# Four heads' output gates moved into the Strassen gate pairs, and the row sums moved to GpSimd

## The chip, the cores and the metric

The program runs on one core of one Trainium2 chip. The metric is the device time of one execution in microseconds (us). Times are medians of several runs; the profile is of one further execution.

In the rows below PE is TensorE's matmul, PEld its weight load, DVE is VectorE, ACT is ScalarE, POOL is GpSimd and SP is SyncE, which here only issues DMAs. "Granted clock" is the share of TensorE's full clock that the chip allowed.

## The reference, cut to what matters

One layer of a hybrid model over 1,280 tokens (1,024 latent and 256 context tokens), width D = 1024, all in float32:

```python
u   = rmsnorm(x, g_norm1) * (1 + sc1) + sh1
xp, su, sv, q, k, v, o_pre, gate_pre, br_pre = split(u @ w_in)
y_a = pool_branch(xp)                                # centred window means, a linear map per group
y_b = su * (w_sgu applied per chunk to rmsnorm(sv))  # spatial gating
h   = mlstm(q, k, v, gate_pre)                       # 4 heads of 128 channels, both directions
h   = rmsnorm_per_head(h) * g_mlstm
y_c = sigmoid(o_pre) * h                             # the output gate of the heads
merged = sum_r sigmoid(br_pre[r]) * (y_r @ w_branch[r])
x  += gt1 * (merged @ w_out)
x  += gt2 * relu(rmsnorm(x)*(1+sc2)+sh2 @ w_ff1)**2 @ w_ff2
```

The change concerns `o_pre` (512 columns of `w_in`, 128 for each head), `br_pre` (3 x 1024 columns) and where `sigmoid(o_pre)` meets `h`.

## The kernel before, in words

Every float32 product is made of three matmuls on rounded parts: a value is split into `hi` (rounded to the matmul's format, by ACT) and `lo` (the rest, by DVE), and hi x hi, hi x lo and lo x hi are summed in PSUM. The modulated input `u` stays on chip, transposed: `uT[k][g]` for 8 blocks k of 128 channels and 3 token groups g of 512, 512 and 256 tokens (the last one is the context).

The stages in order of time:

- Start, 0 to 84 us: modulation, transposes, and the first projections, with an order written out by hand.
- Gate chain, about 84 to 142 us: the heads' input and forget gates, a serial chain of ACT and DVE instructions on 36 partitions (lines 435 to 490, in rows of the tile `z`), then transposes `pc` (line 498).
- Heads, about 142 to 450 us: `head(h)` for h = 0 to 3. Each transposes k and v (`tk`, `tv`), runs the state scan (`kv`, line 607 on DVE), and then for each token group g the scores `st`, the decay rows `rb`, the weights `w` and `e` (lines 635 to 645), the products `pv` (lines 654 and 656), a normalisation whose power is done by POOL (`rs_h`, line 130), the transposes `th` (line 671) and `yc`, which goes to memory. `head_proj(h + 1)` makes the next head's k, v and q with `proj` and `dense` (matmuls of lines 123 to 125, tiles `p_k`, `p_v`, `p_q`); these do not depend on `head(h)` and run between its instructions. So does `proj(I_O + h, ...)` (tile `p_o`), whose sigmoid (line 617) is kept in `so`, a region of `z`, until `yc` is made (line 673).
- After the heads, 450 to 559 us: `sv`'s normalisation, pooling (`pool_project`, `pool_window`, `pool_out`), spatial gating (`spatial`). `quarter_sums` reads `u` back from memory (`scr_u`) into `z` and makes sums of its quarters on DVE (line 800); `split_sum` splits them (lines 809 and 810).
- Gate pairs, 559 to 858 us: 12 objects `GatePair`, each for two blocks of 128 columns of `br_pre`. A pair treats its 256 columns and the 1,024 latent tokens as 2 x 2 blocks and forms them with Strassen's seven block products: `B11`, `B21`, `B22` with parts of `uT` itself, and `T1` to `T4` with the split sums. The context tokens are multiplied in the ordinary way (`contexts`). In between, `mod_piece` multiplies and adds rows of `w_ada` on DVE (lines 539 and 541), 64 pieces, no more than 6 for each pair so far.
- Branches, 858 to 1026 us: for each r, `y_r` is read from memory and split, multiplied by `w_branch[r]` and by the stored gate.
- Output projection, feed-forward with Strassen products, final norm: to 1941 us.

The order of instructions on each engine is that of the program's own scheduler, which runs a model of the engines when the kernel is built (`schedule_with_timeline_sim=True`); it may bring an instruction that is ready ahead of earlier code. Only the start is pinned. Each engine then runs its queue in that fixed order. Tiles of 128 x 512 (`slot`) come from a pool of 59; `uT` holds 40 of them.

Of the kernel before, what the change touches and what calls it, by code (L numbers as in the profile page):

```python
# [7 lines left out]
F32 = mybir.dt.float32  # L8
# [13 lines left out]
H = 4  # L22
# [26 lines left out]
def hybrid_step(  # L49
# [503 lines left out]
    vaug = z[:, 1280:2570].rearrange("p (c t) -> p c t", t=129)  # L553
    vs = z[:, 2570:5150].rearrange("p (c d t) -> p c d t", d=2, t=129)
    S = z[:, 5150:7730].rearrange("p (c d t) -> p c d t", d=2, t=129)
    so = z[:, 7730:9010]
    hn2 = [z[:, 9010 + i * 512 : 9522 + i * 512].rearrange("p (c t) -> p c t", t=P) for i in range(2)]

    def proj(idx, name, evict, eng=V, w=None, groups=range(3)):
# [15 lines left out]
    def head(h, kT, vT, qT):  # L575
# [36 lines left out]
            V.scalar_tensor_tensor(fin[:, d, :], S[:, nx, d, :], dc(nx, d), kv(nx, d), ALU.mult, ALU.add)  # L612
        A.dma_start(st_out[h], fin)

        def ev_o(g, ps):
            t0, n = GROUPS[g]
            A.activation(so[:, t0 : t0 + n], ps[:, :n], AF.Sigmoid)

        ssq = small([P, 16], f"ssq{h}")
        for g in range(3):  # L620
            t0, n = GROUPS[g]
# [41 lines left out]
                V.scalar_tensor_tensor(hn[:, cl, :], pvv[:, 1, 0:P], den[:, 1, :], hn[:, cl, :], ALU.mult, ALU.add)  # L663
                A.activation(vs[:, c, 0, 0:P], hn[:, cl, :], AF.Square, accum_out=ssq[:, c : c + 1])
            r = rstd_of(ssq[:, c0 : c0 + ncn], ncn, f"h{h}_{g}")
            if g == 0:
                proj(I_O + h, f"o{h}", ev_o)
            ps = ps_sd(f"th{h}_{g}")
            for cl in range(ncn):
                A.activation(hn[:, cl, :], hn[:, cl, :], AF.Copy, scale=r[:, cl : cl + 1])  # L670
                PE.transpose(ps[:, cl * P : (cl + 1) * P], hn[:, cl, :], ident)  # L671
            yc = tmp(f"yc{h}_{g}")
            V.scalar_tensor_tensor(  # L673
                yc[:, :n], ps[:, :n], ccol[:, C_GM + h : C_GM + h + 1], so[:, t0 : t0 + n], ALU.mult, ALU.mult)
# [116 lines left out]
    SUMS = {"T1": "B11", "T3": "B12", "T2": "B22", "T4": "B21"}  # L791

    def quarter_sums(raw):
        for kk in range(4):
            b11, b21, b12, b22 = raw["B11"][kk], raw["B21"][kk], raw["B12"][kk], raw["B22"][kk]
            if raw is u_raw:
                for t, k, g in ((b11, kk, 0), (b12, kk, 1), (b22, kk + 4, 1), (b21, kk + 4, 0)):
                    SP.dma_start(t, scr_u[g][k])
            for out, x, y in ((b11, b12, b11), (b12, b22, b12), (b22, b22, b11), (b21, b22, b21)):
                V.tensor_tensor(out, x, y, ALU.subtract)  # L800

    def split_sum(dst, raw, nm):
        for kk in range(4):
            t = raw[SUMS[nm]][kk]
            if nm == "T2" and kk < 3:
                hi, lo = (six(f"t2{i}{kk}") for i in "hl")
            else:
                hi, lo = slot(f"{nm}h{kk}"), slot(f"{nm}l{kk}")
            A.copy(hi, t)
            V.tensor_tensor(lo, t, hi.bitcast(F32), ALU.subtract)  # L810
            dst[nm, kk] = hi, lo

    us = {}
    u_raw = {
        nm: [zs(i) for i in at]
        for nm, at in (("B21", (0, 1, 2, 3)), ("B22", (4, 5, 6, 7)), ("B12", (8, 9, 10, 11)), ("B11", (12, 13, 16, 17)))}
# [45 lines left out]
    pool_out(1)  # L862
    spatial(2)
    pool_out(0)
    quarter_sums(u_raw)

    def early_sums():
        split_sum(us, u_raw, "T4")
        split_sum(us, u_raw, "T3")

    spatial(3, early_sums)

# [113 lines left out]

    ORDER = (1, 0, 2)
    scr_g = [[dp.tile([P, T], F32, name=f"scr_g{r}_{d}") for d in range(KT)] for r in range(3)]

    class GatePair(Pair):  # L990
        def done(self, t):
# [53 lines left out]
    for ri, r in enumerate(ORDER):  # L1045
        scr = (scr_ya, scr_yb, scr_yc)[r]
        ys = [[] for _ in range(4)]
        for g in range(3):
            for kc in range(4):
                t0, n = GROUPS[g]  # L1050
                raw = tmp2(f"yr{r}_{kc}_{g}")
                SP.dma_start(raw[:, :n], scr[kc, :, t0 : t0 + n])
                hi, lo = split_part(f"y{r}_{kc}", g)
                A.copy(hi, raw[:, :n])
                V.tensor_tensor(lo, raw[:, :n], hi.bitcast(F32), ALU.subtract)
                ys[kc].append((hi, lo))
        for d in range(KT):
            if d % 2 == 0:
                wb = [load_half(w_branch[r, d // 2][:, i * 512 : i * 512 + 512], f"wb{r}_{d}_{i}") for i in range(2)]
            for g in range(3):  # L1060
                t0, n = GROUPS[g]
                sg = slot(f"sg{r}_{d}_{g}", F32)
                SP.dma_start(sg[:, :n], scr_g[r][d][:, t0 : t0 + n])
                pb = ps_sd(f"pb{r}_{d}_{g}")
                for kc in range(4):
                    yh, yl = ys[kc][g]
                    whi, wlo = wb[kc // 2]
# [3 lines left out]
                    PE.matmul(pb[:, :n], whi[:, s], yl, start=False, stop=False)  # L1071
# [484 lines left out]
```

## Time and profile before

| | us |
|---|---|
| median of 3 runs | 1944.16 (1943.91 to 1946.34) |
| the profiled execution | 1943.31 |
| its span, first to last instruction | 1941.3 |
| PE busy in the span | 1908.4 (98%) |
| DVE busy | 1287.9 (66%) |
| ACT busy | 856.7 (44%) |
| POOL busy | 382.1 (20%) |

Matmuls are pipelined: a matmul of 512 columns is shown with 0.39 us, but the next one starts 0.23 us later. So a busy share of 98% does not say by itself that PE could go no faster; starts of neighbouring matmuls do.

### The profile page before, as it was taken

The page shows a single profiled execution, that of the slowest core. Times are in us where ns is not written, and L with a number is a line of the kernel's source. Part 1 is how long each engine was busy: PE and PEld are TensorE (multiplying, and loading weights), DVE is VectorE, ACT ScalarE, POOL GpSimd, SP SyncE. Part 2 cuts the span into 40 slices and gives each one's busy share as a digit, 9 for nine tenths or more (in the row PEclk, how much of TensorE's full clock was granted, in tenths as well). Part 3 has the DMA queues.
Part 4 walks back from the last instruction along what each step waited for, and adds up shares of the span by engine and source line. Part 5 has one row for each costly group of instructions (what it writes and reads, how often), then busy time and mean ns, then how long its engine had stood idle before and what let it go on. Part 6 is the DMA issues. An engine that isn't in the chain of part 4 may idle for free.

```text
span 1941.3 us, 28162 instructions
## 1 busy us (share of the span) xinstructions
PE 1908.4 (98%) x10166; PEld 1632.5 (84%) x10166; DVE 1287.9 (66%) x2200; ACT 856.7 (44%) x1760; POOL 382.1 (20%) x381
## 2 busy tenths in 40 slices
PE   8999999999999999999999999999999999999998
PEld 5878888998788888888888888888888888888886
DVE  6574443447759899875675599887876655754665
ACT  6444454653243333343123375555454544443443
POOL 1100001108202424230000005554431210000003
PEclk9999999999999999999999999999999999999999
DMA  9210111012635445459532435777774596654444
GB/s 370 77 60 33 45 38 39 28 57 68 204 125 168 151 151 161 157 195 328 164 103 98 151 121 200 275 263 264 250 256 139 193 335 203 210 168 152 165 133 160
DMA packets 149318, 313.33 MB, mean 161 GB/s; under 512 B 17550, under 2 KB 40818, under 8 KB 147130
## 3 DMA queue, kind: packets, MB, share of 16 engines
q1 hardware_dynamic: 107354, 220.73, 34.6%
q0 software_dynamic: 15520, 57.75, 7.8%
q10 hardware_dynamic: 26304, 33.04, 4.7%
q8 instruction: 80, 1.31, 0.3%
q14 instruction: 60, 0.49, 0.1%
HBM read 217.59 MB, written 93.36 MB: 160 GB/s over the span
## 4 chain that ended last, share of the span: by engine, by line
PE 87%; DVE 6%; ACT 2%; issue 2%; DMA 2%; POOL 1%; SPq 0%; ACTq 0%; POOLq 0%; DVEq 0%
PE w L1423 6%; PE w L1424 6%; PE w L1425 6%; PE fT L912 3%; PE fT L910 3%; PE fT L911 3%; PE pb L1071 3%; PE pb L1070 3%; PE pb L1072 3%; PE fB L911 2%; PE fB L910 2%; PE fB L912 2%; PE fT_g L912 2%; PE fT_g L910 2%; PE fT_g L911 2%; PE po L1190 2%
## 5 line engine op out<-in xcount | busy, mean ns | idle before, releaser
L1262 POOL TENSOR_TENSOR z<-z 128x512 f32<-128x512 f32 x64 | 100.6, 1572 | 119.6 <-DMA z<-in_w_ff 110.1
L967 DVE TENSOR_TENSOR z<-z 128x512 f32<-128x512 f32 x112 | 94.2, 841 | 2.5
L547 POOL PARTITION_ALL_REDUCE acc<-acc x16 | 54.4, 3435 | 183.4 <-DVE acc L541 114.3
L541 DVE SCALAR_TENSOR_TENSOR acc<-z,scond,acc 128x512 f32<-128x512 f32 x112 | 84.6, 803 | 0.1
L1377 POOL TENSOR_TENSOR rs_y<-rs_y,neghalf 128x1 f32<-128x1 f32 x10 | 9.7, 967 | 332.2 <-DVE rs_y L1376 332.1
L1228 ACT ACTIVATE z<-z 128x512 f32<-128x512 f32 x64 | 40.5, 632 | 75.7 <-DVE z L976 38.4
L992 ACT ACTIVATE z<-z 128x512 f32<-128x512 f32 x48 | 30.3, 632 | 54.2 <-DVE z L976 20.6
L130 POOL TENSOR_TENSOR rs_h<-rs_h,neghalf 128x4 f32<-128x4 f32 (+1 forms) x12 | 10.9, 909 | 200.0 <-DVE rs_h L129 199.8
L673 DVE SCALAR_TENSOR_TENSOR yc<-th,ccol,z 128x512 f32<-128x512 f32 (+1 forms) x12 | 7.9, 661 | 58.4 <-PE th L671 58.4
L1076 DVE TENSOR_TENSOR sg<-pb,sg 128x512 f32<-128x512 f32 (+1 forms) x48 | 28.8, 601 | 26.6 <-PE pb L1072 26.4
L901 ACT CAST hi_wb<-raw_wb 128x512 fp32r<-128x512 f32 x24 | 14.7, 620 | 64.0 <-PE pb L1071 37.9
L1229 ACT ACTIVATE z<-z 128x512 f32<-128x512 f32 x64 | 40.3, 629 | 1.1
L1191 DVE TENSOR_TENSOR po<-po,gt 128x512 f32<-128x512 f32 (+1 forms) x24 | 14.6, 609 | 35.6 <-PE po L1190 31.2
L548 POOL TENSOR_TENSOR acc<-acc,bt 1x512 f32<-1x512 f32 x16 | 26.2, 1651 | 59.1 <-issue 59.1
L1253 POOL DMA_DIRECT2D scr_s<-x x48 | 26.3, 550 | 52.4 <-DVE x L1247 46.6
L758 POOL TENSOR_TENSOR z<-z 128x1024 f32<-128x1024 f32 (+13 forms) x20 | 33.6, 1702 | 7.7 <-ACT z L742 5.4
L1194 ACT ACTIVATE po<-z 128x512 f32<-128x512 f32 (+1 forms) x24 | 12.7, 530 | 48.6 <-DVE z L1193 34.3
L607 DVE SCALAR_TENSOR_TENSOR z<-z,dmb,kv 128x129 f32<-128x129 f32 x56 | 16.6, 345 | 21.8 <-PE kv L596 21.3
L1077 DVE TENSOR_TENSOR z<-z,sg 128x512 f32<-128x512 f32 (+1 forms) x48 | 28.7, 602 | 1.2
L660 DVE TENSOR_TENSOR den<-den,gcol 128x2 f32<-128x2 f32 x40 | 6.2, 160 | 31.0 <-ACT den L659 29.9
L130 POOL TENSOR_TENSOR rs_f<-rs_f,neghalf 128x4 f32<-128x4 f32 (+1 forms) x3 | 3.3, 1092 | 116.9 <-DVE rs_f L129 116.9
L654 PE MATMUL pv<-z,w 128*128 128x129 f32 x160 | 25.1, 275 | 0.9 <-DVE w L638 0.9
(5142 smaller groups left out, 7274.1 us busy)
## 6 DMA issues: line engine op xcount, KB each, us to landing
z<-in_w_ff SPq DMA_DIRECT2D x64, 512.0 KB, 5.3
z<-in_w_ada SPq DMA_DIRECT2D x64, 256.0 KB, 3.4
scr_t<-z POOLq DMA_DIRECT2D x16, 1024.0 KB, 4.3
z<-in_w_in SPq DMA_DIRECT2D x24, 512.0 KB, 4.3
scr_g<-z ACTq DMA_DIRECT2D x48, 256.0 KB, 2.0
sg<-scr_g SPq DMA_DIRECT2D x48, 256.0 KB, 4.5
scr_h<-z ACTq DMA_DIRECT2D x48, 256.0 KB, 3.5
scr_s<-x POOLq DMA_DIRECT2D x48, 256.0 KB, 3.8
```

What stands on the lines that cost most here:

```text
L541: V.scalar_tensor_tensor(acc[j], raw, scond[:, k, j : j + 1], acc[j], ALU.mult, ALU.add)
L910: PE.matmul(ps, whi[:, s], ahi, start=first and k == ks[0], stop=False)
L911: PE.matmul(ps, whi[:, s], alo, start=False, stop=False)
L912: PE.matmul(ps, wlo[:, s], ahi, start=False, stop=end and k == ks[-1])
L967: V.tensor_tensor(out, x, y, op)
L1070: PE.matmul(pb[:, :n], whi[:, s], yh, start=kc == 0, stop=False)
L1071: PE.matmul(pb[:, :n], whi[:, s], yl, start=False, stop=False)
L1072: PE.matmul(pb[:, :n], wlo[:, s], yh, start=False, stop=kc == 3)
L1262: G.tensor_tensor(out, x, y, ALU.subtract)
L1423: PE.matmul(banks[j], h_[:, s], rh, start=fp == 0, stop=False)
L1424: PE.matmul(banks[j], l_[:, s], rh, start=False, stop=False)
L1425: PE.matmul(banks[j], h_[:, s], rl, start=False, stop=fp == NFP - 1)
```

## The change

1. The projections `p_o` leave `head`. `yc` is now made by ACT from `th` and `g_mlstm` alone.
2. The four blocks of `o_pre` become two more `GatePair`s, numbers 12 and 13, at the end of the list; their sigmoids go to memory (`scr_o`).
3. In the branch r = 2 the stored `sigmoid(o_pre)` is read beside `y_c` and multiplied in by DVE before the split.
4. `quarter_sums` of `u` becomes `row_sums(h)`, written after each `head(h)`: on POOL, in halves of 256 columns, 8 loads, 8 subtractions and 2 stores for each head, in the region of `z` that `so` had, with the sums stored to memory (`scr_q`). `row_split` then reads a sum straight into the `lo` tile and splits it there.
5. `mod_piece` may run 5 pieces for each pair so far instead of 6.

`quarter_sums` and `split_sum` themselves move down unchanged for the feed-forward part.

```diff
@@ head
-            if g == 0:
-                proj(I_O + h, f"o{h}", ev_o)
...
-            V.scalar_tensor_tensor(
-                yc[:, :n], ps[:, :n], ccol[:, C_GM + h : C_GM + h + 1], so[:, t0 : t0 + n], ALU.mult, ALU.mult)
+            A.activation(yc[:, :n], ps[:, :n], AF.Copy, scale=ccol[:, C_GM + h : C_GM + h + 1])
...
+    scr_q = dp.tile([P, 4, 4, 512], F32, name="scr_q")
+
+    def row_sums(kk):
+        q = z[:, 7730 : 7730 + 1024].rearrange("p (q c) -> p q c", c=256)
+        b21, b22, b12, b11 = (q[:, i, :] for i in range(4))
+        for hf in range(2):
+            c = slice(hf * 256, hf * 256 + 256)
+            for t, k, g in ((b11, kk, 0), (b12, kk, 1), (b22, kk + 4, 1), (b21, kk + 4, 0)):
+                G.dma_start(t, scr_u[g][k][:, c])
+            for out, x, y in ((b11, b12, b11), (b12, b22, b12), (b22, b22, b11), (b21, b22, b21)):
+                G.tensor_tensor(out, x, y, ALU.subtract)
+            G.dma_start(scr_q[:, :, kk, c], q)
...
         head(h, *cur)
+        row_sums(h)
...
+    def row_split(nm, i):
+        for kk in range(4):
+            room = six if nm == "T2" and kk < 3 else slot
+            hi, lo = room(f"{nm}h{kk}"), room(f"{nm}l{kk}")
+            SP.dma_start(lo.bitcast(F32), scr_q[:, i, kk, :])
+            A.copy(hi, lo.bitcast(F32))
+            V.tensor_tensor(lo, lo.bitcast(F32), hi.bitcast(F32), ALU.subtract)
+            us[nm, kk] = hi, lo
...
-    quarter_sums(u_raw)
     def early_sums():
-        split_sum(us, u_raw, "T4")
-        split_sum(us, u_raw, "T3")
+        row_split("T4", 0)
+        row_split("T3", 2)
...
-    NGP = 3 * KT // 2
+    GATES = [(I_BR + r * KT + d, scr_g[r][d : d + 2]) for r in ORDER for d in range(0, KT, 2)]
+    GATES += [(I_O + h, scr_o[h : h + 2]) for h in range(0, H, 2)]
+    NGP = len(GATES)
...
-        while n > 0 and piece < 64 and piece < 6 * n:
+        while n > 0 and piece < 64 and piece < 5 * n:
...
+                if r == 2:
+                    so = tmp2(f"so{kc}_{g}")
+                    SP.dma_start(so[:, :n], scr_o[kc][:, t0 : t0 + n])
+                    V.tensor_tensor(raw[:, :n], raw[:, :n], so[:, :n], ALU.mult)
```

More of the change, by code (lines that the diff above doesn't have):

```diff
@@ L555, in hybrid_step @@
     S = z[:, 5150:7730].rearrange("p (c d t) -> p c d t", d=2, t=129)
-    so = z[:, 7730:9010]
     hn2 = [z[:, 9010 + i * 512 : 9522 + i * 512].rearrange("p (c t) -> p c t", t=P) for i in range(2)]
@@ L613, in head @@
         A.dma_start(st_out[h], fin)
-        def ev_o(g, ps):
-            t0, n = GROUPS[g]
-            A.activation(so[:, t0 : t0 + n], ps[:, :n], AF.Sigmoid)
         ssq = small([P, 16], f"ssq{h}")
@@ L786, in pool_out @@
             SP.dma_start(scr_ya[gi, :, t0 : t0 + n], ya[:, :n])
-    SUMS = {"T1": "B11", "T3": "B12", "T2": "B22", "T4": "B21"}
-    def quarter_sums(raw):
+    def row_split(nm, i):
         for kk in range(4):
[L795 to L811, printed above, removed]
+            room = six if nm == "T2" and kk < 3 else slot
[4 more added lines that the diff above has]
+            us[nm, kk] = hi, lo
     us = {}
-    u_raw = {
-        nm: [zs(i) for i in at]
-        for nm, at in (("B21", (0, 1, 2, 3)), ("B22", (4, 5, 6, 7)), ("B12", (8, 9, 10, 11)), ("B11", (12, 13, 16, 17)))}
     wst = z[:, 9216:9728].rearrange("p (g c) -> p g c", c=P)
@@ L988, in hybrid_step @@
     scr_g = [[dp.tile([P, T], F32, name=f"scr_g{r}_{d}") for d in range(KT)] for r in range(3)]
+    scr_o = [dp.tile([P, T], F32, name=f"scr_o{h}") for h in range(H)]
     class GatePair(Pair):
@@ L995, in context_done, with store @@
             A.activation(t, ps, AF.Sigmoid)
-        def store(self, r, d):
+        def store(self, dsts):
             for f, (t1, t2) in enumerate(((self.a1, self.a2), (self.b1, self.b2))):
-                dst = scr_g[r][d + f]
+                dst = dsts[f]
                 A.dma_start(dst[:, 0:512], t1)
@@ L1005, in hybrid_step @@
         us["B11", kk], us["B21", kk], us["B22", kk] = uT[kk][0], uT[kk + 4][0], uT[kk + 4][1]
-    NGP = 3 * KT // 2
     gates = {}
+    GATES = [(I_BR + r * KT + d, scr_g[r][d : d + 2]) for r in ORDER for d in range(0, KT, 2)]
+    GATES += [(I_O + h, scr_o[h : h + 2]) for h in range(0, H, 2)]
+    NGP = len(GATES)
     def gate_pair(n):
-        r, d = ORDER[n // 4], n % 4 * 2
-        i = I_BR + r * KT + d
+        i = GATES[n][0]
         odd = n % 2
@@ L1018, in hybrid_step @@
     gates[0].begin()
-    split_sum(us, u_raw, "T2")
+    row_split("T2", 1)
     gate_pair(1)
     gates[1].begin()
-    split_sum(us, u_raw, "T1")
+    row_split("T1", 3)
     for n in (0, 1):
@@ L1031, in hybrid_step @@
         gates[n].rest()
-        gates[n].store(ORDER[n // 4], n % 4 * 2)
+        gates[n].store(GATES[n][1])
         del gates[n]
-        while n > 0 and piece < 64 and piece < 6 * n:
+        while n > 0 and piece < 64 and piece < 5 * n:
             mod_piece(piece, zs((12, 13, 16, 17)[piece % 4]))
@@ L1129, in hybrid_step, with quarter_sums, split_sum @@
     V.scalar_tensor_tensor(a2, a2, 1.0, g2v, ALU.add, ALU.mult)
+    SUMS = {"T1": "B11", "T3": "B12", "T2": "B22", "T4": "B21"}
+    def quarter_sums(raw):
+        for kk in range(4):
+            b11, b21, b12, b22 = raw["B11"][kk], raw["B21"][kk], raw["B12"][kk], raw["B22"][kk]
+            for out, x, y in ((b11, b12, b11), (b12, b22, b12), (b22, b22, b11), (b21, b22, b21)):
+                V.tensor_tensor(out, x, y, ALU.subtract)
+    def split_sum(dst, raw, nm):
+        for kk in range(4):
+            t = raw[SUMS[nm]][kk]
+            if nm == "T2" and kk < 3:
+                hi, lo = (six(f"t2{i}{kk}") for i in "hl")
+            else:
+                hi, lo = slot(f"{nm}h{kk}"), slot(f"{nm}l{kk}")
+            A.copy(hi, t)
+            V.tensor_tensor(lo, t, hi.bitcast(F32), ALU.subtract)
+            dst[nm, kk] = hi, lo
     raw2 = [[None] * KT for _ in range(2)]
```

## The prediction

> **What bounds the kernel now.** I read the page's busy shares first, then PE's waits over the whole run, then the busy times by stage, then single matmuls.
>
> ```profile
> PE 1908.4 (98%) x10166; PEld 1632.5 (84%) x10166; DVE 1287.9 (66%) x2200; ACT 856.7 (44%) x1760; POOL 382.1 (20%) x381
> ```
>
> PE is shown busy for 98% of the span. What it waited for, longest first (total, times, longest):
>
> ```profile
> PE pc L498 <- DVE z L486: 3.6, 1, 3.6
> ...
> PE fT_g L912 <- DVE s_g7l L893: 1.7, 1, 1.7
> ...
> PE sv L698 <- ACT sv L702: 1.2, 1, 1.2
> PE p_xp L123 <- DVE mt L842: 1.1, 1, 1.1
> ...
> PE pv L654 <- DVE w L638: 0.9, 1, 0.9
> ...
> PE p_k L123 <- ACT z L617: 0.7, 1, 0.7
> ```
>
> Stretches of the run: the gate chain, the heads one by one (two left out), the gate pairs.
>
> ```profile
> core 0: us, PE busy (x) PEld busy (x) DVE busy (x) ACT busy (x) POOL busy (x), PEclk, DMA share, GB/s
> 84.00:142.00 58.00, 53.62 (x308) 47.08 (x309) 42.86 (x63) 25.37 (x34) 2.46 (x5) 0.94 0.17 50
> 142.00:218.00 76.00, 76.00 (x466) 67.49 (x465) 34.11 (x101) 37.37 (x103) 2.76 (x3) 1.00 0.13 42
> ...
> 559.00:858.00 299.00, 295.56 (x1569) 254.80 (x1568) 255.67 (x362) 116.46 (x212) 98.21 (x60) 1.00 0.46 148
> ```
>
> So PE is the bound in both places that the change touches. In the first head (142 to 218 us) it never pauses, with DVE and ACT each under half busy. In the gate pairs DVE is at 255.67 of 299 us, 86%, and once holds PE up (1.7 us). The one large wait is at the end of the gate chain. Hence the sum starts with matmuls removed and added.
>
> **The change part by part. Projections removed.** First and last of 12 consecutive 512-column matmuls of one `p_o`, then of its 24 context matmuls of 256 columns:
>
> ```profile
> 179.83 0.39 PE L123 MATMUL p_o<-u4h,hi_o 128*128 128x512 f32 x1
> ...
> 182.32 0.39 PE L125 MATMUL p_o<-u7h,lo_o 128*128 128x512 f32 x1
> ...
> 189.81 0.28 PE L123 MATMUL p_o<-u0c,hi_o 128*128 128x256 f32 x1
> ...
> 192.57 0.28 PE L125 MATMUL p_o<-u7c,lo_o 128*128 128x256 f32 x1
> ```
>
> A step is 2.49 / 11 = 0.226 us and 2.76 / 23 = 0.120 us. One `p_o` is 48 x 0.226 + 24 x 0.120 = 13.7 us; four are 55.0 us.
>
> **Pairs added.** A pair is 7 products x 12 = 84 matmuls of 512 and 48 of 256 columns: 24.7 us by those steps. Measured, the same DVE addition of the fourth and of the eleventh pair, seven pairs apart:
>
> ```profile
> 664.11 0.68 DVE L983 TENSOR_TENSOR z<-z,fB_g 128x512 f32<-128x512 f32 x1
> ...
> 838.46 0.68 DVE L983 TENSOR_TENSOR z<-z,fB_g 128x512 f32<-128x512 f32 x1
> ```
>
> 174.35 / 7 = 24.9 us. I take 24.9 since the row has the pair's own waits in it; two pairs are +49.8 us. The gain on PE is one product in eight of the latent part: 55.0 - 49.8 = 5.2 us.
>
> **DVE in the pairs.**
>
> ```profile
> L541 DVE SCALAR_TENSOR_TENSOR acc<-z,scond,acc 128x512 f32<-128x512 f32 x112 | 84.6, 803 | 0.1
> L800 DVE TENSOR_TENSOR z<-z x16: 684/686/694, 498.7 to 524.2; 128x512 f32<-128x512 f32 x16
> ```
>
> One piece less per pair takes 2 x 0.80 = 1.6 us of DVE out of 24.9. Against the 1.7 us wait I credit -1.0 us (between 0 and -1.7). The 16 subtractions of line 800, 11.0 us of DVE, go too; PE's only waits around them are 1.1 us (`mt`), so I credit nothing, at most -1.1. The slower spreading of pieces still ends with the last pair, since 5 x 13 > 64.
>
> **Splits from memory.**
>
> ```profile
> L810 DVE TENSOR_TENSOR T4l<-z,T4h x4: 684/688/692, 524.8 to 542.7; 128x512 fp32r<-128x512 f32 x4
> ...
> L910 PE MATMUL fT_g<-T4h,a_g0h x4: 389/394/400, 576.0 to 582.6; 128*128 128x512 f32 x4
> ...
> z<-scr_u SPq DMA_DIRECT2D x16, 256.0 KB, 3.9
> ```
>
> Loads now come after the tile is free, not before. If all 16 began only at 542.7, when the last `T4` got its tile, one landing (3.9) and 16 splits (16 x 0.69 = 11.0) end at 557.6, before 576.0, where the first is used. So the cost is nothing; the cover is `begin` and `contexts` of two pairs. Without it, 3.9 us once. The loads stand in SP's queue ahead of the pairs' weights; a load that waits for its tile holds those back, which the same slack covers.
>
> **The last branch.**
>
> ```profile
> L1055 DVE TENSOR_TENSOR y_3c<-yr,y_3c x3: 417/417/419, 865.4 to 931.9; 128x256 fp32r<-128x256 f32 x3
> ...
> L1071 PE MATMUL pb<-y_3l,hi_wb x48: 389/389/389, 864.0 to 1025.0; 128*128 128x512 f32 x48
> ```
>
> Twelve multiplications (8 x 0.69 + 4 x 0.42 = 7.2 us) and twelve more loads precede the splits of r = 2, which ended at 931.9; the third branch starts two thirds of the way from 864.0 to 1025.0, near 971. The 39 us between hide them: 0, else +7.2.
>
> **The gate chain.**
>
> ```profile
> 131.62 2.31 PE L498 MATMUL pc<-cst,z 36*128 36x36 f32 x20 [3.62 <-DVE z L486]
> 133.87 0.58 PE L125 MATMUL p_k<-u4c,lo_k 128*128 128x256 f32 x1
> ...
> 136.16 0.63 PE L123 MATMUL p_v<-u0h,hi_v 128*128 128x512 f32 x1
> 136.59 0.63 PE L124 MATMUL p_v<-u0l,hi_v 128*128 128x512 f32 x1
> ```
>
> Here PE's queue reaches `pc` before DVE has made its input. The wait is 3.62 us and more: the ten matmuls from 133.87 to 136.16 take 2.29 us instead of 1.20, and about four more take 0.43 instead of 0.23, so the pause costs 3.6 + 1.9 = 5.5 us. The first `p_o` stood ahead of it; the next head's projections take its place, so I leave the pause as it is. What is new is POOL: `row_sums` needs nothing of the heads, only `scr_u` and its part of `z`, so it may start here, not beside the heads.
>
> ```profile
> L758 POOL TENSOR_TENSOR z<-z 128x256 f32<-128x256 f32 x4 | 3.4, 860 | 2.3 <-ACT z L743 2.2
> ...
> L776 POOL TENSOR_TENSOR xp<-z,xp 128x256 f32<-128x256 f32 x4 | 7.3, 1837 | 0.3
> ...
> L183 POOL DMA_DIRECT2D scr_u<-val_u x16: 542/573/674, 27.5 to 69.1; - x16
> ```
>
> A POOL subtraction of 128 x 256 takes 0.86 to 1.84 us: 32 of them 27.5 to 59 us, and 40 DMA issues of 0.57 us 23 us, on an engine that is nearly idle. But POOL and DVE get in each other's way: ten equal DVE operations beside POOL's additions took between 0.47 and 2.62 us,
>
> ```profile
> L707 DVE TENSOR_SCALAR vn<-vn,rs_v x10: 469/854/2622, 446.6 to 458.0; 128x512 f32<-128x512 f32 x10
> ...
> 446.56 8.63 POOL L758 TENSOR_TENSOR z<-z 128x1216 f32<-128x1216 f32 x5
> ...
> 446.63 10.45 DVE L707 TENSOR_SCALAR vn<-vn,rs_v 128x512 f32<-128x512 f32 x8 [1.85 <-POOL rs_v L130]
> ```
>
> so a POOL subtraction inside the chain can lengthen it by its own time. With none there the cost is 0, with all eight of head 0 8 x 0.86 = 6.9 us. I take two, +1.7 us, nearer the low end: a half's four loads must land before its subtractions, and its store must leave before the next half loads.
>
> The Trainium skill, GPSIMD Engine Reference, Key points, says that GpSimd shares its SBUF interfaces with VectorE and contends with VectorE instructions that have two SBUF inputs or run in a 2-port mode. The trace agrees (0.47 against 2.62 us); taken as full exclusion it puts all eight into the sum, which becomes +1.7 us.
>
> **The heads.** Table switches of ACT, the product `yc` and the power `rs_h` there:
>
> ```profile
> L617 ACT ACT_TABLE_LOAD x10 | 12.8, 1283 | 1.5 <-DVE z L446 1.4
> ...
> L637 ACT ACT_TABLE_LOAD x9 | 11.5, 1283 | 2.5 <-DVE fin L612 2.4
> ...
> L673 DVE SCALAR_TENSOR_TENSOR yc<-th,ccol,z x12: 473/750/752, 186.6 to 458.4; 128x512 f32<-128x512 f32 x8, 128x256 f32<-128x256 f32 x4
> ...
> L130 POOL TENSOR_TENSOR rs_h<-rs_h,neghalf x12: 697/1007/1043, 179.7 to 443.2; 128x4 f32<-128x4 f32 x8, 128x2 f32<-128x2 f32 x4
> ```
>
> `rs_h` (about 1 us, 12 times) now shares POOL's queue with loads and subtractions. If it stands behind a subtraction that waits for its load, ACT's scaling, `th` and everything behind `th` in PE's queue wait with it; the splits of `sv`'s weights, also POOL's, come after all four `row_sums` and are late only if these are. `yc` costs ACT about what its sigmoid did and frees DVE of 12 times 0.47 to 0.75 us; neither engine bounds. The other loss is cover: 13.7 us less work per head that PE can do while a head's chain runs.
>
> Against this the chain itself gets shorter: 19 switches between sigmoid and exp, 24.3 us of ACT, and twelve sigmoids go. In the first head 76 - 13.7 = 62 us of PE work stay beside 34 us of DVE and 37 us of ACT, which partly overlap. So PE should stay the bound, and I take +1.0 us; the bounds are -2.8 (the waits on `sv`, `pv` and line 617 in the list above go) and +16.5 (one pause of 5.5 us in each of heads 0 to 2).
>
> Sum: -55.0 + 49.8 - 1.0 + 1.7 + 1.0 = -3.5 us. The profiled execution took 1943.3 us, which gives 1939.8 us; the median of the runs shown, 1944.16 us, is 0.9 us above it. A change of 0.2% (3.9 us) is about what can be told from none, so the forecast, 4.4 us below the median, is only just a gain.
>
> **The rivals.** *Lost cover, slower.* In heads 0 to 2 PE runs out of projections and pauses at `pv` or `th`, each pause at the price seen at `pc`, 5.5 us. For it: the gate chain uses up the next head's projections early, and `uT` leaves 19 tiles of 59 for the heads. Against it: 62 us of PE work per head. One pause eats the gain; three give 1943.3 - 6.2 + 16.5 = 1953.6 us. From two pauses and a half on (1950.9 and beyond) it is surely slower; the bound is 1948.1. The Trainium skill, TensorE: Matmul & The Clock Gate, says that an idle window of about 3.4 us halves TensorE's clock until a busy one has passed; the 0.43 us steps behind the 3.62 us pause agree, and shorter pauses would cost only themselves.
>
> *POOL in the gate chain, no change.* All eight subtractions of head 0 fall in it: 1943.3 - 6.2 + 6.9 + 1.0 = 1945.0 us. For it: DVE works there without a break; against it: loads must land and stores must leave between the halves.
>
> *The waits go too, faster.* With the table switches gone and POOL out of the way, the waits on `sv`, `pv`, line 617, `mt` and the pair's 1.7 us vanish: 1943.3 - 5.2 - 1.7 - 2.8 - 1.1 = 1932.5 us.
>
> **How the numbers follow.** Forecast 0.45, lost cover 0.18, POOL 0.20, waits gone 0.17. The forecast's own range is 1936 to 1942; four fifths of it lie below 1940.3. Faster: 0.36 + 0.17 = 0.53. Same: 0.09 + 0.18 = 0.27 (a tenth of POOL's case turns slower). Slower: 0.18 + 0.02 = 0.20. The range, 1932 to 1950, leaves out most of the three-pause case and a little below.
>
> **What would show it.** `p_o` gone and fourteen pairs 24.6 to 24.9 us apart; the first pair starting about 53 us earlier, near 506; no wait of PE on `T` splits; line 541's stretch without the 1.7 us wait. Lost cover would show as PE waits on `w`, `e` or `rs_h` with a granted clock below 1 between 142 and 400 us; POOL in the chain as a longer wait at `pc` and POOL subtractions before 132 us. I am wrong if the scheduler lays out the later stages differently, or if the first pair starts later than 512.

## The result: 0.5% slower, and the profile after

The changed kernel takes 1953.9 us (median of 4 runs, 1951.8 to 1955.0) against 1944.2 us (4 runs, 1943.9 to 1946.3): a ratio of 1.0049, 95% interval 1.0037 to 1.0061. The forecast of 1939.8 us was wrong in sign, and the time lies 4 us above the range. The profiled execution of the changed kernel took 1954.9 us with a span of 1953.1 us.

The page's busy shares look almost as before. PE is still 98% busy, which shows how little that share says here:

```profile
PE 1909.8 (98%) x10142; PEld 1633.3 (84%) x10142; DVE 1303.4 (67%) x2218; ACT 848.7 (43%) x1771; POOL 437.0 (22%) x453
```

What PE waited for, over the whole run (total, times, longest), is another list than before:

```profile
PE pc L498 <- DVE z L486: 7.1, 1, 7.1
PE th L664 <- ACT z L663: 6.3, 3, 4.5
PE pv L649 <- DVE w L633: 3.3, 2, 1.6
...
PE fB_g L898 <- ACT a_g0h L880: 2.3, 1, 2.3
```

`th` is new, `pv` has grown from 0.9, `pc` from 3.6, and the first gate pair, `fB_g`, now starts with a pause. The busy times by stretch say where. First the changed kernel, head by head (144 to 408 us), then the time to the first pair, then the pairs:

```profile
core 0: us, PE busy (x) PEld busy (x) DVE busy (x) ACT busy (x) POOL busy (x), PEclk, DMA share, GB/s
...
144.00:227.00 83.00, 83.00 (x502) 73.73 (x502) 33.67 (x98) 33.87 (x102) 39.65 (x57) 1.00 0.39 127
227.00:287.00 60.00, 57.65 (x393) 52.23 (x391) 26.75 (x90) 30.18 (x99) 9.89 (x6) 1.00 0.13 43
287.00:342.00 55.00, 46.82 (x360) 44.97 (x360) 29.13 (x91) 30.99 (x113) 5.96 (x4) 0.91 0.11 37
342.00:408.00 66.00, 65.99 (x486) 62.39 (x485) 29.31 (x84) 36.73 (x125) 7.35 (x15) 1.00 0.11 37
408.00:518.00 110.00, 107.71 (x585) 91.28 (x584) 76.92 (x82) 34.24 (x62) 50.44 (x42) 1.00 0.43 142
518.00:868.00 350.00, 349.83 (x1850) 302.28 (x1851) 279.95 (x407) 138.98 (x254) 93.78 (x60) 1.00 0.44 146
```

and the kernel before, its four heads, in the same columns:

```profile
142.50:218.50 76.00, 76.00 (x463) 67.53 (x463) 33.85 (x100) 37.68 (x104) 2.76 (x3) 1.00 0.13 40
218.50:298.50 80.00, 79.31 (x477) 69.65 (x476) 33.46 (x97) 39.70 (x107) 2.71 (x3) 1.00 0.12 39
298.50:373.00 74.50, 72.34 (x516) 67.45 (x515) 28.81 (x93) 41.28 (x122) 9.89 (x6) 1.00 0.11 35
373.00:440.00 67.00, 67.00 (x526) 64.87 (x525) 30.50 (x87) 38.25 (x126) 5.52 (x8) 1.00 0.13 44
```

Before, the heads (bounded here by the first transposes of each) took 76, 80, 74.5 and 67 us, and PE paused for 2.9 us in all. After, they take 83, 60, 55 and 66 us: the first is longer although 13.7 us of work has left it, and in the second and third PE pauses for 2.35 and 8.18 us, the third at a granted clock of 0.91. DVE and ACT are busy for 41 to 56% of the changed kernel's heads, so no engine took PE's place as the bound: in its pauses PE was waiting for a chain of instructions on several engines.

Two rows of each kernel bound the stages: the first and the last matmul of the gate pairs, before

```profile
558.57 0.40 PE L910 MATMUL fB_g<-u0h,a_g0h 128*128 128x512 f32 x1
...
861.77 0.39 PE L912 MATMUL fB_g<-u7h,s_g11l 128*128 128x512 f32 x1
```

and after:

```profile
517.91 0.79 PE L898 MATMUL fB_g<-u0h,a_g0h 128*128 128x512 f32 x1 [2.29 <-ACT a_g0h L880]
...
868.20 0.39 PE L900 MATMUL fB_g<-u7h,s_g13l 128*128 128x512 f32 x1
```

With the same rows further on, the balance is:

| stage | before, us | after, us | change | forecast |
|---|---|---|---|---|
| start to the first pair | 558.6 | 517.9 | -40.7 | -55.0 + 1.7 + 1.0 = -52.3 |
| gate pairs | 303.2 | 350.3 | +47.1 | +49.8 - 1.0 = +48.8 |
| branches, output projection | 282.3 | 282.3 | 0.0 | 0 |
| feed-forward to the last matmul | 789.4 | 792.5 | +3.2 | 0 |
| last matmul to the end of the span | 7.8 | 10.1 | +2.3 | 0 |
| span | 1941.3 | 1953.1 | +11.8 | -3.5 |

So 11.6 us are missing ahead of the first pair, 5.5 us were lost behind the pairs in places that the forecast did not touch, and the pairs came out 1.7 us better than forecast.

### The profile page after: what moved, and what is told of

Read it like the earlier page. It is cut to its first block, busy times and chain, and to the rows that moved or that the text cites. A ratio compares the mean times of both kernels' runs of the same rounds, so it can differ in the third digit from the quotient of the medians.

```text
span 1953.1 us, 28281 instructions
## 1 busy us (share of the span) xinstructions
PE 1909.8 (98%) x10142; PEld 1633.3 (84%) x10142; DVE 1303.4 (67%) x2218; ACT 848.7 (43%) x1771; POOL 437.0 (22%) x453
## 4 chain that ended last, share of the span: by engine, by line
PE 77%; DMA 2%; POOL 2%; ACT 1%; DVE 1%; issue 1%; POOLq 0%; SPq 0%; ACTq 0%; DVEq 0%
PE w L1436 6%; PE w L1437 6%; PE w L1438 6%; PE pb L1065 3%; PE pb L1064 3%; PE pb L1066 3%; PE fT_g L898 3%; PE fT L900 3%; PE fT L898 3%; PE fT_g L899 3%; PE fT L899 3%; PE fT_g L900 3%; PE fB L899 2%; PE fB L900 2%; PE fB L898 2%; PE fB_g L898 2%
## 5 line engine op out<-in xcount | busy, mean ns | idle before, releaser
L1241 ACT ACTIVATE z<-z 128x512 f32<-128x512 f32 x64 | 40.4, 632 | 76.4 <-DVE z L964 37.0
L981 ACT ACTIVATE z<-z 128x512 f32<-128x512 f32 x56 | 35.3, 631 | 62.3 <-DVE z L964 17.3
L630 DVE SCALAR_TENSOR_TENSOR w<-rb,gcol,cst 128x128 f32<-128x128 f32 x80 | 21.9, 344 | 37.2 <-PE rb L626 37.1
L766 POOL TENSOR_TENSOR z<-z 128x256 f32<-128x256 f32 (+13 forms) x20 | 37.4, 1875 | 17.6 <-ACT z L751 11.0
L1242 ACT ACTIVATE z<-z 128x512 f32<-128x512 f32 x64 | 40.2, 629 | 1.1
L548 POOL TENSOR_TENSOR acc<-acc,bt 1x512 f32<-1x512 f32 x16 | 22.1, 1392 | 58.3 <-issue 58.3
L681 POOL TENSOR_TENSOR z<-z 128x256 f32<-128x256 f32 x32 | 31.1, 973 | 8.8 <-DMA z<-scr_u 6.9
L679 POOL DMA_DIRECT2D z<-scr_u x32 | 17.3, 550 | 64.2 <-PE p_k L125 45.5
L130 POOL TENSOR_TENSOR rs_h<-rs_h,neghalf 128x4 f32<-128x4 f32 (+1 forms) x12 | 11.8, 987 | 88.6 <-DVE rs_h L129 88.3
```

## The experiments

Three theories for the 11.6 us. **Cover**: PE ran out of independent projections beside the heads' chains. **Kind of cover**: what is left to cover them, `sv`, brings its own ACT casts, evictions and POOL splits into the chains' way. **GpSimd**: the row sums on POOL hold up the chains or the gate chain. Each run below says how far the first gate pair lies behind where the pure change of PE's work would put it ("loss": for the changed kernel 517.9 - (558.6 - 55.0) = 14.3 us). Ratios are against the kernel before, timed in the same set of runs; the stage times are each of one profiled execution.

### The gating alone, without the row sums on POOL (e_gates)

`row_sums`, `row_split` and `scr_q` are out, `quarter_sums` and `split_sum` on DVE are back as before:

```diff
-        row_sums(h)
...
+    quarter_sums(u_raw)
...
-        row_split("T4", 0)
+        split_sum(us, u_raw, "T4")
```

> The output gates as two more pairs, but the row sums made as before (on DVE behind the pooling, no work of GpSimd beside the heads). Cover theory (PE pauses in the heads because p_o is gone): the pauses at th and pv stay; only the longer wait at pc (7.1 against 3.6 us) and the longer drain of GpSimd at the end (6.4 against 2.5 us) go back: about 1949 us. GpSimd theory (its row sums delay DVE and rs_h): all pauses go, about 1939 to 1940 us. Theory of sv's splits (sv now starts in head 2, and its weights' splits on GpSimd stand ahead of rs_h): the 4.7 us pause at th stays, the rest goes, about 1944 us.

Measured: 1949.4 us, ratio 1.0033 (1.0020 to 1.0046). The pauses in the heads stand unchanged to a tenth of a microsecond:

```profile
PE th L664 <- ACT z L663: 6.3, 3, 4.5
PE pc L498 <- DVE z L486: 5.6, 1, 5.6
PE pv L649 <- DVE w L633: 3.3, 2, 1.6
```

So the row sums do not make them, and the time is the 1949 us that goes with lost cover, not the 1939 to 1940 us of the GpSimd theory or the 1944 us of that of `sv`'s splits. Three things went with the row sums: the pause at the first gate pair (2.3 to 0.4 us), 1.3 us of the gate chain and 2.3 us at the end of the program (both below).

### The row sums without their subtractions, and without POOL's DMAs (e_nosub, e_spdma)

One kernel leaves out the 32 subtractions on POOL, so that the sums hold unsubtracted quarters; the other lets SP issue the 40 transfers.

```diff
@@ e_nosub
-                G.tensor_tensor(out, x, y, ALU.subtract)
@@ e_spdma
-                G.dma_start(t, scr_u[g][k][:, c])
+                SP.dma_start(t, scr_u[g][k][:, c])
...
-            G.dma_start(scr_q[:, :, kk, c], q)
+            SP.dma_start(scr_q[:, :, kk, c], q)
```

> The changed kernel without the 32 subtractions on GpSimd (its loads and stores stay, so the quarters and not their sums are stored: that part of the computation is left out). GpSimd theory: DVE's scans in the gate chain run at their old times, the wait at pc goes back from 7.1 to about 3.6 us: about 1950 us. Cover theory and theory of sv's splits: within 1 us of the changed kernel in the heads; a gain at pc alone of 3.5 us is not excluded by them, one in the heads is.

> The changed kernel with the 40 DMAs of the row sums issued by SP instead of GpSimd; the subtractions stay on GpSimd. GpSimd theory: its drain at the end goes back from 6.4 to about 2.5 us, which takes some 2.3 us off the span: about 1951 us; if queueing behind the issues also held rs_h, more. Cover theory and theory of sv's splits: the drain aside, nothing changes; they make no claim on the drain.

Measured: 1952.9 us (1.0042, 1.0026 to 1.0059) and 1953.0 us (1.0049, 1.0034 to 1.0064). In both, `th` waits 6.3 us and `pv` 3.3 us, as in the changed kernel. The row sums on GpSimd are rejected as the cause of the heads' loss. Neither median reached the time that the GpSimd theory gave it (about 1950 and 1951 us). What the subtractions do cost is seen in the gate chain. POOL in the changed kernel:

```profile
114.53 2.14 POOL L679 DMA_DIRECT2D z<-scr_u  x4 [45.53 <-PE p_k L125]
...
118.18 1.71 POOL L681 TENSOR_TENSOR z<-z 128x256 f32<-128x256 f32 x1
...
120.19 3.47 POOL L681 TENSOR_TENSOR z<-z 128x256 f32<-128x256 f32 x2
...
126.39 2.39 POOL L681 TENSOR_TENSOR z<-z 128x256 f32<-128x256 f32 x1
```

As the prediction had it, the sums start in the gate chain and not beside their head: four subtractions of head 0 lie there. From the start of line 445 to the end of line 486 on DVE the chain takes 22.7 us, without the subtractions 21.8 us, in the kernel before 21.4 us. That is +1.3 us for all of `row_sums`, 0.9 of it for the subtractions.

### The splits of `sv`'s weights moved from POOL to DVE (e_svdve, e_gates_sv)

The longest pause, in head 2 of the changed kernel, in order of time, all engines:

```profile
325.48 0.23 ACT L659 ACTIVATION_READ_ACCUMULATOR z<-z 128x1 f32 x1
325.58 1.07 ACT L93 CAST hi_sv<-raw_sv 128x1024 fp32r<-128x1024 f32 x1
326.51 0.35 ACT L659 ACTIVATE z<-z 128x128 f32<-128x128 f32 x1
...
326.72 2.34 POOL L94 TENSOR_TENSOR lo_sv<-raw_sv,hi_sv 128x1024 fp32r<-128x1024 f32 x1 [11.80 <-ACT hi_sv L93]
...
327.56 1.54 DVE L129 TENSOR_SCALAR rs_h<-ssq 128x4 f32<-128x4 f32 x1 [1.73 <-ACT z L659]
329.01 1.21 DVE L94 TENSOR_TENSOR lo_xp<-raw_xp,hi_xp 128x1024 fp32r<-128x1024 f32 x1
...
329.17 1.91 POOL L130 TENSOR_TENSOR rs_h<-rs_h,neghalf 128x4 f32<-128x4 f32 x1
331.12 0.99 ACT L663 ACTIVATE z<-z,rs_h 128x128 f32<-128x128 f32 x3 [2.66 <-POOL rs_h L130]
331.58 0.47 PE L664 MATMUL th<-cst,z 128*128 128x128 f32 x1 [4.53 <-ACT z L663]
```

ACT is in the middle of the four squares that `rs_h` needs when a cast of `sv`'s weights, 1.07 us, comes between. The split `lo_sv` then stands on POOL while DVE's tiny `rs_h` of 128 x 4 needs 1.54 us instead of the usual 0.17 (the median of its 12), and `rs_h` on POOL takes 1.91 us instead of the usual 1.0. PE's queue stands at `th` meanwhile: the first half of `sv` is done, and the second needs the split that POOL is making. The edit, made in the changed kernel and in the kernel with the gating alone:

```diff
-        wq = [load_w(w_sv[q, hf], f"sv{q}_{hf}", eng=G) for hf in range(2)]
+        wq = [load_w(w_sv[q, hf], f"sv{q}_{hf}", eng=V) for hf in range(2)]
```

> The changed kernel with the split of sv's weights (four subtractions of 128 x 1024) on DVE instead of GpSimd. Theory of sv's splits: the waits of PE at th (6.3 us in all) go, about 1948 us. Cover theory and GpSimd theory: still 1952 to 1955 us, the pauses only move.

> The output gates as two more pairs, row sums as before, sv in its place, but the splits of sv's weights on DVE. Kind of cover: the longest pause at th goes from 4.5 to about 2.5 us, as it did with the row sums on GpSimd; about 1946 us. Amount of cover: 1949 us, as without the edit.

Measured: 1950.1 us (1.0041, 1.0028 to 1.0054) and 1944.3 us (0.9998, 0.9989 to 1.0007). The waits in the second:

```profile
PE th L664 <- ACT z L663: 4.4, 3, 2.6
PE pc L498 <- DVE z L486: 4.2, 1, 4.2
PE pv L649 <- DVE w L633: 3.3, 2, 1.6
```

The longest pause falls from 4.5 to 2.6 us, the others stay: as the theory of kind had it in the second run, while in the first the theory of `sv`'s splits had all of `th`'s 6.3 us going, and 1.7 us went. The loss ahead of the first pair falls from 14.3 to 10.8 us in the changed kernel, and from 13.2 to 7.3 us with the gating alone. Not all of that is the edit's. The gate chain (line 445) begins at another time in each profile, between 109.3 and 111.4 us, although no edit touches the code ahead of it, and in these two it began 1.6 and 1.8 us earlier than in the kernels they are compared with. Without this the loss falls by 2.0 and 4.1 us. So the kind of cover is a part of the loss, 2 to 4 us of it by these profiles, but not all: over half of it remains with these splits off POOL. The casts of `sv` on ACT are still there, so the rest need not be the amount alone.

### The dead projection put back (e_cover)

The changed kernel with `p_o` at its old place, its result evicted by ACT onto itself and not used:

```diff
+            if g == 0:
+                proj(I_O + h, f"o{h}", lambda gg, pp: A.copy(pp[:, : GROUPS[gg][1]], pp[:, : GROUPS[gg][1]]))
```

> The changed kernel with the four p_o projections put back into the heads as dead work (PE does them, ACT copies the sums in place, nobody reads them). It costs 55 us of PE. Cover theory, in both its forms below: with p_o back sv starts in head 3 again, the waits of PE at th and pv (9.6 us) go, and the run takes some 1998 us (1954 + 55 - 11). GpSimd theory: the waits stay, 1954 + 55 = 2009 us.

Measured once: 1997.3 us, as the cover theories had it (1998) and 12 us from the GpSimd theory's 2009. The first pair starts at 559.4 us, where 55.0 us of added work would put it at 572.9. The list of PE's waits between 100 and 700 us:

```profile
PE pc L498 <- DVE z L486: 6.8, 1, 6.8
PE fB_g L900 <- ACT a_g0h L882: 2.2, 1, 2.2
PE th L666 <- ACT z L665: 0.7, 1, 0.7
```

With the row sums, the `sv` splits on POOL and everything else of the change in place, the waits at `pv` go and 0.7 us is left at `th`. Putting 55.0 us of work on PE costs 41.4 us ahead of the first pair: 13.6 us of the 14.3 are cover. This run decides against the row sums on GpSimd. It can't tell the two cover theories apart, since `sv` starts at 342.6 us again and so leaves heads 1 and 2.

### Other cover in its place (g_xp2, g_xp2_sv)

The gating alone, with two projections that come after the heads, `pool_project(3)` and `(2)` (13.7 us each), written ahead of `sv`; the second also with the splits on DVE.

```diff
+    pool_project(3)
+    pool_project(2)
     vn = []
...
-    pool_project(3)
-    pool_project(2)
```

> The output gates as two more pairs, the row sums as in the kernel before (on DVE behind the pooling), and the first two pooling projections (p_xp) written ahead of sv's, so that p_xp takes p_o's place as PE's work beside the last heads. Amount of cover: the work is the same in sum, the pauses at th and pv (9.6 us) stay, about 1949 us. Kind of cover: sv's work holds the heads up by what it asks of ACT (two evictions for every 24 short matmuls, casts) and of GpSimd and DVE (splits); p_xp asks for little; the pauses go, 1938 to 1941 us.

> As the run before, with the splits of sv's weights on DVE. Kind of cover: no slower than it, 1937 to 1941 us, since no subtraction of GpSimd meets DVE beside the heads. Amount of cover: about 1948 us.

Measured: 1948.4 us (1.0014, 1.0005 to 1.0023) and 1948.7 us (1.0020, 1.0011 to 1.0029). In the first, `sv` starts at 311.9 instead of 273.4 us, the waits at `th` become four of at most 1.4 us and `pv` 1.6; but a new wait stands where the two projections were (the same in the second run):

```profile
PE mx L826 <- DVE vn L715: 3.5, 3, 1.8
```

The loss is 11.3 us, against 13.2, and in the second run 11.7 us, against 7.3 without the move. Both times are those of the theory of amount (about 1949 and 1948 us), not the 1937 to 1941 us of the theory of kind, although part of the waits at `th` and `pv` did go (9.6 to 5.9 us). What was borrowed from the stage after the heads was missing there.

### Half of the gates in a pair (e_half, e_half_early, e_keep03, e_keep13)

From the gating alone with the splits on DVE: two heads' `o` go into one pair, the two heads in `KEEP` keep `p_o`, its sigmoid in `so` and the product; `mod_piece` may run 6 pieces for each pair, as in the kernel before. With heads that are no neighbours, the line of `GATES` names the two others instead. On PE this is -27.5 + 24.9 = -2.6 us against the kernel before.

```diff
+    KEEP = (2, 3)      # (0, 1) in e_half_early, (0, 3) in e_keep03, (1, 3) in e_keep13
...
+            if g == 0 and h in KEEP:
+                proj(I_O + h, f"o{h}", ev_o)
...
-    GATES += [(I_O + h, scr_o[h : h + 2]) for h in range(0, H, 2)]
+    GATES += [(I_O + h, scr_o[h : h + 2]) for h in range(0, H, 2) if h not in KEEP]
...
-                if r == 2:
+                if r == 2 and kc not in KEEP:
```

> Only the o of heads 0 and 1 goes into a Strassen pair; heads 2 and 3 keep p_o, its sigmoid and the product in the head. Row sums and subtractions as in the kernel before, the splits lo_sv on VectorE. On PE that is -27.5 + 24.9 = -2.6 us against the kernel before; thirteen pairs, six pieces per pair as before, so no relief of VectorE there. Theory cover, filler is one stock (PE takes independent projections as early as it can, and it is the total left that decides): half of the stock that was taken away is back, the waits of th and pv fall from 4.4 + 3.3 us to 0 to 3 us, 1941.8 to 1945 us, and the kernel that keeps heads 0 and 1 instead comes out alike, within 2 us and with the same waits. Theory place (only work that belongs to heads 2 and 3 can cover them): no wait at th or pv here, 1941.8 us, and the kernel that keeps heads 0 and 1 has these waits in full and takes 1945 us or more.

> The mirror: only the o of heads 2 and 3 goes into a Strassen pair; heads 0 and 1 keep p_o, its sigmoid and the product. Otherwise as the kernel that keeps heads 2 and 3: -2.6 us on PE against the kernel before. Theory cover, one stock: the p_o of heads 0 and 1 lets the projections of the later heads stand longer, sv starts later, the waits of th and pv are as small as in the other half (0 to 3 us), 1941.8 to 1945 us. Theory place: heads 2 and 3 stay without cover, the waits of th and pv are 4 + 3 us as with all four in pairs, 1945 to 1948 us.

Measured: 1957.8 us (1.0069, 1.0056 to 1.0081) with heads 2 and 3 kept, 1943.9 us (0.9993, 0.9984 to 1.0002) with heads 0 and 1 kept. Neither theory had the first: one stock of filler said that the two come out alike, place said that the late one is better. Its rows tell why (the timeline, all engines, head 2's first group; the `p_o` is that of head 3):

```profile
304.63 0.28 PE L125 MATMUL p_o<-u7c,lo_o 128*128 128x256 f32 x1
...
327.66 0.75 DVE L675 SCALAR_TENSOR_TENSOR yc<-th,ccol,z 128x512 f32<-128x512 f32 x1 [5.03 <-PE th L672]
...
328.45 0.60 ACT L618 ACTIVATE z<-p_o 128x512 f32<-128x512 f32 x1 [2.12 <-DVE yc L675]
...
329.10 0.39 PE L704 MATMUL sv<-hi_sv,u0h 128*128 128x256 f32 x1 [1.47 <-ACT z L618]
```

PE had taken head 3's `p_o` a whole head early. Its sigmoid could not be written before head 2's `yc` had read the one `so`, the PSUM banks of `p_o` stayed full for 24 us, and `sv`, which needs such a bank, could not begin. Work taken early covered nothing and shut out what would have covered. The two further choices of `KEEP` have no neighbours:

> The o of heads 1 and 2 as one Strassen pair, heads 0 and 3 keep p_o, sigmoid and product; otherwise as the two halves (on PE -2.6 us against the kernel before). The half that kept heads 2 and 3 lost 12 us in head 2: p_o of head 3 was done by 304.8 us, but its sigmoid, into the one tile so, stood behind head 2's product yc until 328.45, p_o held its PSUM banks, and sv began at 329.1 right behind that sigmoid. Theory banks: with no two neighbours among the kept heads the tile so is free when p_o ends, sv starts when the projections end, the th and pv waits are at most those of the half that kept heads 0 and 1 (2.5 + 1.6 us), first gate pair at 531 to 534 us, 1941.5 to 1944.5 us. Theory place (late p_o is poor cover whatever holds its banks): waits of th and pv of 5 us and more in heads 2 and 3, first gate pair at 538 us or later, 1949 us or more.

> The o of heads 0 and 2 as one Strassen pair, heads 1 and 3 keep p_o, sigmoid and product; otherwise as the halves. Theory banks: no two neighbours among the kept heads, so no p_o that waits for the tile so with its banks held; first gate pair at 531 to 534 us, th and pv waits at most 2.5 + 1.6 us, 1941.5 to 1944.5 us. Theory place: the kept p_o are later than in the kernel that keeps 0 and 3, so it is worse: 1949 to 1957 us with 5 us and more at th and pv.

Measured: 1946.6 us (1.0017, 1.0008 to 1.0025) and 1949.1 us (1.0021, 1.0012 to 1.0031; its runs spread from 1944.2 to 1951.5 us, and the profiled one took 1945.5 us). In both profiles `sv` begins at 301 to 303 us and the waits at `th` and `pv` are at most 3.0 and 1.6 us, much as with heads 0 and 1 kept (2.5 and 1.6). That is what the banks theory forecast for the heads, and the 5 us and more of the place theory are not there. The times do not follow it: 1946.6 us lies between the two theories' windows, 1949.1 us in that of place, and with heads 0 and 3 kept the first pair starts at 539.5 us, where place had it (538 or later). In that profile the missing time is not at `th` or `pv`: the gate chain began 1.2 us late, PE waited 2.9 us at `mx`, and behind this the clock was granted at 0.50 for 3.4 us. With 1 and 3 kept the profiled execution was one of the two fastest of ten and does not show what the slower ones lost. So the held banks are shown as what kept `sv` out in the late half; that place plays no part in the time is not shown.

The losses ahead of the first gate pair in one table, each against that kernel's own work on PE:

| kernel | first pair at, us | by PE's work | loss | gate chain begins later by |
|---|---|---|---|---|
| changed kernel | 517.9 | 503.6 | 14.3 | 0.8 |
| changed, no subtractions on POOL | 516.8 | 503.6 | 13.2 | -0.4 |
| changed, row-sum transfers on SP | 517.8 | 503.6 | 14.2 | -0.4 |
| changed, `sv` splits on DVE | 514.4 | 503.6 | 10.8 | -0.8 |
| changed, dead `p_o` put back | 559.4 | 558.6 | 0.8 | 0.5 |
| gating alone | 516.8 | 503.6 | 13.2 | 1.2 |
| gating alone, two `xp` earlier | 514.9 | 503.6 | 11.3 | -0.2 |
| gating alone, `sv` splits on DVE | 510.9 | 503.6 | 7.3 | -0.7 |
| the same, two `xp` earlier | 515.2 | 503.6 | 11.7 | -0.5 |
| `sv` splits on DVE, heads 0 and 1 keep `p_o` | 534.0 | 531.1 | 2.9 | -0.2 |
| the same, heads 1 and 3 keep `p_o` | 534.5 | 531.1 | 3.4 | 0.0 |
| the same, heads 0 and 3 keep `p_o` | 539.5 | 531.1 | 8.4 | 1.2 |
| the same, heads 2 and 3 keep `p_o` | 543.9 | 531.1 | 12.8 | 1.2 |

The last column is part of the loss and not of the edit, so two losses compare to about 2 us. Half of the cover given back takes the loss from 7.3 to about 3 us in two of the four choices of heads, and to 8.4 and 12.8 us in the two others; all of it back takes the changed kernel's 14.3 to 0.8. No version is measurably faster than the kernel before: the best, with heads 0 and 1 kept, has 0.9993 with an interval that holds 1.

### The end of the program

From SP's issue of the last output transfer to the end of the span it takes 3.2 us in the kernel before (1938.1 to 1941.3), 5.4 us in the changed one (1947.7 to 1953.1) and 3.1 us in the one whose row-sum transfers SP issues (1948.5 to 1951.6). Behind this stands POOL's closing drain, which the trace records but does not count as busy. Its three records (shortest, median and longest, in ns) in these kernels, in that order:

```profile
L1547 POOLq DRAIN  x3: 52/99/2462, 1936.3 to 1941.0; - x3
L1560 POOLq DRAIN  x3: 52/99/6381, 1945.9 to 1952.8; - x3
L1560 POOLq DRAIN  x3: 52/99/2463, 1946.7 to 1951.3; - x3
```

The longest is 6.38 us in all four profiles in which POOL issues the 40 transfers of `row_sums`, and 2.46 us in the ten others, that with these transfers on SP among them. So this 2.3 us is the price of POOL's DMA issues, some 1,700 us after the last of them landed (213.8 us). The run with the transfers on SP is hardly faster for it; in its profile the feed-forward part took 795.4 us instead of 792.5.

## Why the prediction was wrong

**The heads' cover is the step that failed.** It was taken at +1.0 us, with bounds of -2.8 and +16.5; the loss that goes when the dead projection is put back is 13.6 us. The argument was that 62 us of PE work stay beside 34 us of DVE and 37 us of ACT in the first head. It went wrong twice. The busy time of a chain's engines is not its length: it hands over between PE, DVE, ACT and POOL, as the rows of the longest pause show, and in the third head PE waited for 8.2 us of 55 with DVE and ACT busy for 29 and 31 us. And an average over heads was used for a stock that is spent in order. Counted by its matmuls and the steps of 0.226 and 0.120 us, the heads of the changed kernel have 64, 37, 23 and 47 us of projections to run (`sv` and `xp` included), those of the kernel before 57, 59, 52 and 48. The first takes its successors' too, so that `sv` begins at 271.8 us instead of 343.0, and the third, with the least, loses most. The prediction named what speaks for it (the gate chain uses up the next head's projections early), and argued it away with the average. Its own sign of being wrong, a first pair later than 512 us, came at 517.9 us. Of the 13.6 us, 2 to 4 are the kind of cover (`sv`'s splits on POOL); how the rest divides between its amount and `sv`'s other work stays open, though the runs with `xp` in `sv`'s place, which gained little or lost, speak for the amount.

The loss can also be added up from PE's side. Its waits between 100 us and the start of the first pair grow from 8.2 to 19.7 us. At a granted clock of 0.50 it was busy for 5.1 us from 128.6 to 138.8 us and 7.0 us from 330.0 to 340.2 us, against 6.3 us from 131.1 to 137.9 us before; taking half of that as lost, an estimate, adds 2.9 us. Together 14.4 us, against a loss of 14.3.

**The rival had it.** Lost cover was given 0.18 and 1953.6 us; the median is 1953.9. The number is right by some luck: not three pauses of 5.5 us in heads 0 to 2 but five at `th` and `pv`, 9.6 us in all, in heads 1 and 2, 3.5 us more at `pc`, and 5.5 us behind the first pair that the rival did not have. The clock of 0.91 from 287 to 342 us is what that rival said would show: 10.2 us at 0.50, from 330.0 us on, which is within the 4.5 us pause. The Trainium skill, TensorE: Matmul & The Clock Gate, What's actually happening, has the clock at half after an idle window of about 3.4 us. The 4.5 us pause agrees, and so does the stretch before it, whose longest pause is 1.6 us and which was granted 1.00. But "shorter pauses would cost only themselves" does not hold. With heads 0 and 1 kept, a pause of 2.5 us, shorter than that window, was followed by the half clock as well, and the measurement decides:

```profile
330.00:340.20 10.20, 6.99 (x31) 6.62 (x32) 4.00 (x15) 5.48 (x20) 1.09 (x1) 0.50 0.39 129
...
348.51 0.48 PE L672 MATMUL th<-cst,z 128*128 128x128 f32 x1 [2.51 <-ACT z L671]
...
348.50:358.70 10.20, 8.57 (x39) 8.20 (x40) 4.11 (x16) 5.52 (x22) 0.70 (x1) 0.50 0.32 113
```

The first row is the changed kernel, the two others are the kernel with heads 0 and 1 kept; the columns are those of the stretches above.

**The wait at `pc`.** "I leave the pause as it is" failed: PE reaches `pc` at 133.70 - 7.10 = 126.6 us, 1.4 us earlier than before (131.62 - 3.62 = 128.0), and `pc` starts 2.1 us later: 1.3 us for the longer chain and 0.8 us for its later begin. The wait grows by 3.5 us.

```profile
133.70 2.32 PE L498 MATMUL pc<-cst,z 36*128 36x36 f32 x20 [7.10 <-DVE z L486]
```

POOL's price in the chain, taken at +1.7 for two subtractions, measured +1.3 with four of them in it.

**Splits from memory.** "So the cost is nothing; the cover is `begin` and `contexts`" failed by 1.9 us. The timeline of the changed kernel, all engines:

```profile
513.51 0.32 SPq L832 DMA_DIRECT2D scr_yb<-mt  x1
...
513.92 0.38 SPq L801 DMA_DIRECT2D T1l<-scr_q  x1
...
516.72 0.62 ACT L802 CAST T1h<-T1l 128x512 fp32r<-128x512 f32 x1 [3.34 <-DMA T1l<-scr_q]
...
517.25 0.61 ACT L880 CAST a_g0h<-z 128x512 fp32r<-128x512 f32 x1
```

The split's first use is late, as the prediction said, but the cast of the split stands in ACT's queue ahead of `a_g0h`, which the first matmul of the first pair needs. The load left late behind a store on SP, the cast waited 3.34 us for it, and `a_g0h` with it. The pause at the first pair is 2.2 to 2.7 us in all five kernels that keep `row_split`, and none of the nine others has it. Whose first use is late can still hold up its neighbour in the queue.

**What was right.** The sum of matmuls: with all `p_o` back the first pair starts at 559.4 us, 0.8 us behind the kernel before, and the pairs take 350.3 / 14 = 25.0 us each. The relief of DVE in the pairs is real and was put too low: PE paused for 3.4 us there before, and for 0.2 us in 350 after. A pair takes 24.9 to 25.0 us in every kernel with 5 pieces for each pair, and 25.2 to 25.3 us in every one with 6. The last branch hides the multiplications and loads: 0.0 us. That `row_sums` may start in the gate chain was right.

**Not foreseen.** 2.3 us of drain at the end, and 3.2 us from the feed-forward part to the last matmul, whose code is unchanged. That stretch took between 790.5 and 795.4 us in the other kernels of this study, against 789.4 before, with the same code in an order that the scheduler lays out anew each time. PE's waits in it are 7.0 us in all, against 6.2 before, and the clock was granted at 0.50 for 6.8 us of it instead of 3.4. What makes the difference was not tested and stays open; each figure is of one execution, and the kernel before alone ranged from 1941.8 to 1948.7 us over 20 runs.

## What to carry to other kernels

Work that an engine does beside a serial chain has two values: its own time and the pauses that it fills. Before taking such work out, find the chain's own length (no run here shows it bare; with 23 us of other work beside it a head took 55 us, not the 34 and 37 us of its engines), count the filler that is left, and follow in which order the scheduler spends it; where a section's filler falls short of the chain, the gain is lost. Filler isn't all alike: one that shares the chain's engines stretches it, and one that cannot be evicted holds the banks that the next one needs.

## What the runs showed of the hardware

In the longest pause, DVE's `rs_h` on 128 x 4 values begins at 327.56 and ends at 329.10 us, when POOL's `lo_sv` has ended at 326.72 + 2.34 = 329.06; its usual time is 0.17 us. Then it is the other way round: POOL's `rs_h` begins at 329.17 beside DVE's `lo_xp`, which lasts until 330.22 us, and ends 0.86 us after it, where it usually takes some 1.0 us in all. So here a tiny operation waited out a large one of the other engine, both ways. The Trainium skill, SBUF — State Buffer, SBUF: two separate sides, states a rule of this kind: of a GpSimd instruction and a VectorE instruction that has two SBUF inputs or runs in a 2-port mode, whichever starts first holds their common ports for the whole instruction. These rows agree; in which mode DVE's `rs_h` ran they do not show. In the gate chain it was mostly POOL that gave way. Its 32 subtractions by shape (shortest, median and longest, in ns):

```profile
L681 POOL TENSOR_TENSOR z<-z x32: 725/742/2393, 118.2 to 209.4; 128x256 f32<-128x256 f32 x32
```

The four of the gate chain (rows above; the middle row holds two of them) took 7.5 us, 4.5 us more than four times the median, and DVE's chain lost 1.3 us, 0.9 of it to the subtractions.

And the time of POOL's closing drain depends on whether it issued these 40 transfers long before: 6.38 against 2.46 us.
